# Low halves of weight tiles: a VectorE subtraction replaced by an accumulating DMA

## The chip, the cores and the metric

The kernel runs on one core of a Trainium2 chip. The metric is the device time of one execution in microseconds (us), a median over runs. Engines: PE (TensorE matmuls; PEld is its weight load), ACT (ScalarE), DVE (VectorE), POOL (GpSimd) and SP (SyncE, which here only issues DMAs). Sixteen DMA engines move all data.

## The reference

One decoder layer on a float32 input of 256 positions by 2048 channels:

```
h = rmsnorm(x); z = h @ w_in                      # 2048 x 7176
a, hb, c = conv module(z), mLSTM(z), gMLP(z)      # 512, 1024, 512 channels
x = x + concat(a, hb, c) @ w_out                  # 2048 x 2048
hm = rmsnorm(x) @ w_up                            # 2048 x 8192
x = x + square(relu(hm)) @ w_down                 # 8192 x 2048
out = rmsnorm(x)
```

## The kernel before

All weights are cut on the host into **tiles** (the code's `pieces`) of 128 x 2048 floats, 1 MB each: 64 for the mixer (numbers 0 to 63), then for each of four quarters `q` of the hidden width 16 tiles of `w_up` and 16 of `w_down`. The `w_up` tiles have numbers 64 + 32q to 79 + 32q; each is one block of 128 columns with all 2048 rows. Two neighbours fill one accumulator in PSUM, and `g` counts these pairs: tile 64 + 32q + 2g and the odd one after it.

The products are made to near float32 precision from float32r operands. Every weight is split into `hi` (rounded to float32r) and `lo` (what is left), and three products are summed. The split is done by half tile, called a **unit** (1024 columns of the tile); unit h belongs to tile h // 2. `split_unit` lets ACT copy the unit to `hi` (L131), and DVE subtracts `hi` from the raw weights to give `lo` (L132). `load_piece` issues a tile's load on SP's queue (L103).

In an up stage `mm_t` (L201 to L226) takes a tile in two halves. The first half does 8 wide matmuls (`hi` against both parts of the activations, 512 columns, L217) and then 8 narrow ones (`lo` against the high part, 256 columns, L222); the second half does its 8 narrow ones first and its 8 wide ones last. So in the trace 16 narrow ones stand together in the middle of a tile, and 16 wide ones across the border of two tiles. After a pair the results are squared behind a ReLU (L675 to L680). In a down stage `mm_n` takes each half tile with 12 matmuls (L240 to L242).

What orders the work: there are 4 buffers for raw tiles, 5 for `hi` and 5 for `lo`. Unit h therefore takes the buffers of unit h - 5, and tile j the raw buffer of tile j - 4. `advance` runs the splits 4 units ahead of the matmuls and the loads as far ahead as buffers allow. The order of the instructions on ACT, DVE, PE and SP is set by a scheduler from priorities (a split has `high_priority(HP)`); POOL keeps program order (`IN_ORDER`). In both MLP stages POOL has nothing to do until the last quarter's closing work (L700).

Of the kernel before, what the change touches and what calls it, by code (L numbers as in the profile page):

```python
# [11 lines left out]
ALU = mybir.AluOpType  # L12
# [12 lines left out]
NQ = 4  # L25
# [5 lines left out]
UNITS = 2  # L31
# [27 lines left out]
def trunk(ctx: ExitStack, tc: tile.TileContext, x, xt, w_t, w_n, w_o, w_u, w_d, gw, gm_w, cols, rows, out):  # L59
    nc = tc.nc  # L60
# [19 lines left out]
    for q in range(NQ):  # L80
        pieces += [w_u[q * 16 + i] for i in range(16)]
        pieces += [w_d[q * 16 + i] for i in range(16)]
    raws, his, los = {}, {}, {}
    state = {"dma": 0, "split": 0, "later": {}}
    n_units = len(pieces) * UNITS
# [23 lines left out]
    def x_prep(k):  # L109
        g = lng[:, k:k + 1]  # L110
        nc.scalar.mul(xg[:, k, 0, :], xs4[:, k, :], g)
        nc.vector.scalar_tensor_tensor(out=xg[:, k, 1, :], in0=xs4[:, k, :], scalar=g,
                                       in1=xg[:, k, 0, :].bitcast(F32), op0=ALU.mult, op1=ALU.subtract)

    def split_unit():

        h = state["split"]
        state["split"] += 1
        parts = 1
        if h < 4 * UNITS:  # L120
            kn = 4 // UNITS
            for k in range(h * kn, (h + 1) * kn):
                x_prep(k)
            parts = 2 if h < P2 else 1
        raw = raws[h // UNITS][:, h % UNITS * UW:(h % UNITS + 1) * UW]
        hi = wpool.tile([P, UW], F32R, tag="hi", name=f"hi{h}")
        lo = wpool.tile([P, UW], F32R, tag="lo", name=f"lo{h}")
        n = UW // parts
        for i in range(parts):
            s = slice(i * n, (i + 1) * n)  # L130
            nc.scalar.copy(hi[:, s], raw[:, s])  # L131
            nc.vector.tensor_tensor(out=lo[:, s], in0=raw[:, s], in1=hi[:, s].bitcast(F32), op=ALU.subtract)  # L132
        his[h], los[h] = hi, lo
        if h % UNITS == UNITS - 1:
            raws.pop(h // UNITS)

    def advance(h):
        while state["dma"] * UNITS <= h + DMA_AHEAD and state["dma"] < len(pieces):
            load_piece()
        while state["split"] <= h + SPLIT_AHEAD and state["split"] < n_units:  # L140
            with tc.high_priority(HP):
                split_unit()
        for fn in state["later"].pop(h, []):
            fn()
# [488 lines left out]
    for c in range(4):  # L633
# [5 lines left out]
        for cp in range(2):  # L639
# [6 lines left out]
            for i in range(2):  # L646
                k = 4 * c + 2 * cp + i
                g = colv[:, C_LMG + k:C_LMG + k + 1]
# [141 lines left out]
```

## Time and profile before

| | |
|---|---|
| median of 3 runs | 1103.77 us (1103.71 to 1104.51) |
| profiled execution | 1103.79 us, of which its span is 1102.1 us |
| PE busy | 1089.6 us, 99% |
| DVE busy | 689.6 us, 63% |
| ACT busy | 530.7 us, 48% |
| POOL busy | 57.8 us, 5% |
| moved by DMA | 211.05 MB, mean 191 GB/s |

The span is the profiled stretch of the execution. Busy shares are means over it; whether an engine sets the time is seen from who waits for whom in a stretch. Idle time of an engine that nobody waits for costs nothing.

### The profile page before, as it was taken

The numbers are of one execution on the slowest core, as the hardware profiler recorded it, in microseconds if no ns is written. First come the engines' busy times: TensorE is split into PE (matmuls) and PEld (weight loads), VectorE is DVE, ScalarE is ACT, GpSimd is POOL, SyncE is SP. The second block draws the span as 40 slices with busy tenths as digits, with TensorE's granted clock in tenths as the row PEclk, the third lists the DMA queues.
The fourth block names the chain that finished last, engine by engine and source line by source line (L and its number), as shares of the span: only waits on it lengthen the run. The fifth ranks groups of instructions, "written<-read, shape, count | busy, mean of one in ns | idle before, by whom it ended". The sixth has DMA issues, their size and how long they took to land.

```text
span 1102.1 us, 13677 instructions
## 1 busy us (share of the span) xinstructions
PE 1089.6 (99%) x5447; PEld 924.1 (84%) x5447; DVE 689.6 (63%) x841; ACT 530.7 (48%) x655; POOL 57.8 (5%) x70
## 2 busy tenths in 40 slices
PE   9999999999999999999999999999999999999997
PEld 7888888888888888888888888888888888888885
DVE  7788999665665556555546565555565555565553
ACT  7574755444564454443334443334444334444442
POOL 1002120040300000000000000000000000000111
PEclk9999999999999999999999999999999999999999
DMA  9645445554475555555555555555555555555531
GB/s 347 261 172 179 167 163 190 182 191 169 175 305 186 180 189 186 187 183 194 194 210 184 186 178 193 196 197 202 186 189 180 194 198 205 189 183 177 196 141 76
DMA packets 32176, 211.05 MB, mean 191 GB/s; under 512 B 3697, under 2 KB 4081, under 8 KB 7665
## 3 DMA queue, kind: packets, MB, share of 16 engines
q1 hardware_dynamic: 32112, 210.19, 54.1%
q8 instruction: 42, 0.69, 0.3%
q14 instruction: 22, 0.17, 0.0%
HBM read 208.08 MB, written 2.10 MB: 191 GB/s over the span
## 4 chain that ended last, share of the span: by engine, by line
PE 90%; DVE 5%; issue 3%; POOL 1%; ACT 1%; DMA 0%; SPq 0%; ACTq 0%; POOLq 0%; DVEq 0%
PE up L217 21%; PE up L222 11%; PE dn L242 10%; PE dn L241 10%; PE dn L240 10%; PE wo L240 3%; PE wo L242 3%; PE wo L241 3%; PE qk L217 2%; DVE lo L132 2%; DVE cvo L313 2%; PE o L240 1%; PE o L242 1%; PE o L241 1%; PE v L241 1%
## 5 line engine op out<-in xcount | busy, mean ns | idle before, releaser
L132 DVE TENSOR_TENSOR lo<-raw,hi 128x1024 fp32r<-128x1024 f32 (+1 forms) x388 | 474.6, 1226 | 340.8 <-ACT hi L131 340.6
L131 ACT CAST hi<-raw 128x1024 fp32r<-128x1024 f32 (+1 forms) x388 | 402.8, 1042 | 449.7 <-PE dn L242 188.7
L217 PE MATMUL up<-x,hi 128*128 128x512 f32 x1024 | 245.6, 391 | 0.0
L217 PEld LDWEIGHTS up<-x,hi 128*128 128x128 f32 x1024 | 188.0, 188 | 36.2
L240 PE MATMUL dn<-hi,u 128*128 128x512 f32 x480 | 186.7, 389 | 0.0
L241 PE MATMUL dn<-lo,u 128*128 128x512 f32 x480 | 186.7, 389 | 0.0
L242 PE MATMUL dn<-hi,u 128*128 128x512 f32 x480 | 186.7, 389 | 0.0
L222 PEld LDWEIGHTS up<-x,lo 128*128 128x128 f32 x1024 | 131.4, 191 | 5.1
L222 PE MATMUL up<-x,lo 128*128 128x256 f32 x1024 | 133.0, 283 | 0.0
L241 PEld LDWEIGHTS dn<-lo,u 128*128 128x128 f32 x480 | 90.1, 188 | 18.8
L240 PEld LDWEIGHTS dn<-hi,u 128*128 128x128 f32 x480 | 90.1, 188 | 18.7
L242 PEld LDWEIGHTS dn<-hi,u 128*128 128x128 f32 x480 | 90.1, 188 | 18.7
L217 PE MATMUL qk<-xg,hi 128*128 128x512 f32 x256 | 62.4, 392 | 1.0 <-DVE qk_t L413 1.0
L217 PEld LDWEIGHTS qk<-xg,hi 128*128 128x128 f32 x256 | 46.7, 188 | 10.9 <-PE qk L217 1.8
L313 DVE SCALAR_TENSOR_TENSOR cvo<-aT,colv,cvo 128x256 f32<-128x256 f32 x120 | 53.9, 498 | 0.0
L240 PE MATMUL wo<-hi,mix 128*128 128x512 f32 x128 | 50.4, 394 | 0.0
L241 PE MATMUL wo<-lo,mix 128*128 128x512 f32 x128 | 50.1, 391 | 0.0
L242 PE MATMUL wo<-hi,mix 128*128 128x512 f32 x128 | 49.9, 390 | 0.0
L700 POOL TENSOR_TENSOR xr<-xr,fgv 128x512 f32<-128x512 f32 x6 | 9.5, 1606 | 765.9 <-ACT jf L698 765.9
L679 ACT CAST u<-u_t 128x512 fp32r<-128x512 f32 x32 | 19.9, 621 | 53.0 <-DVE u_t L678 53.0
L680 DVE TENSOR_TENSOR u<-u_t,u 128x512 fp32r<-128x512 f32 x32 | 22.1, 691 | 19.3 <-ACT u L679 19.3
L222 PEld LDWEIGHTS qk<-xg,lo 128*128 128x128 f32 x256 | 32.9, 191 | 1.3
(224 smaller groups left out, 1006.5 us busy)
## 6 DMA issues: line engine op xcount, KB each, us to landing
raw<-in_w_u SPq DMA_DIRECT2D x64, 1024.0 KB, 4.7
raw<-in_w_d SPq DMA_DIRECT2D x64, 1024.0 KB, 4.7
raw<-in_w_n SPq DMA_DIRECT2D x28, 1024.0 KB, 4.7
raw<-in_w_t SPq DMA_DIRECT2D x16, 1024.0 KB, 4.7
raw<-in_w_o SPq DMA_DIRECT2D x16, 1024.0 KB, 4.8
raw<-in_w_n SPq DMA_DIRECT2D x6, 512.0 KB, 7.6
xr<-in_x SPq DMA_DIRECT2D x2, 1024.0 KB, 6.5
out<-xr SPq DMA_DIRECT2D x8, 256.0 KB, 2.6
```

Source lines behind the costliest of these rows:

```text
L131: nc.scalar.copy(hi[:, s], raw[:, s])
L132: nc.vector.tensor_tensor(out=lo[:, s], in0=raw[:, s], in1=hi[:, s].bitcast(F32), op=ALU.subtract)
L217: nc.tensor.matmul(pt[:, i, :], lhsT=hi[:, kk, :], rhs=act[:, k, :, :], start=(k == 0), stop=(k == NK - 1))
L222: nc.tensor.matmul(pt[:, i, 0:T], lhsT=lo[:, kk, :], rhs=act[:, k, 0, :], start=False, stop=False)
L240: nc.tensor.matmul(pt[t], lhsT=xh, rhs=hi[:, kk, :], start=(k == 0), stop=False)
L241: nc.tensor.matmul(pt[t], lhsT=xh, rhs=lo[:, kk, :], start=False, stop=False)
L242: nc.tensor.matmul(pt[t], lhsT=xl, rhs=hi[:, kk, :], start=False, stop=(k == NK - 1))
L313: nc.vector.scalar_tensor_tensor(out=o, in0=a, scalar=w, in1=o, op0=ALU.mult, op1=ALU.add)
L679: nc.scalar.copy(u[:, 2 * g:2 * g + 2, 0, :], tt)
L680: nc.vector.tensor_tensor(out=u[:, 2 * g:2 * g + 2, 1, :], in0=tt, in1=u[:, 2 * g:2 * g + 2, 0, :].bitcast(F32), op=ALU.subtract)
L700: nc.gpsimd.tensor_tensor(out=xr[:, t, cs], in0=xr[:, t, cs], in1=fgv[:, cs], op=ALU.mult)
```

## The change

For the odd `w_up` tile of each pair (32 tiles, 64 units) the low part is no longer a DVE subtraction. ACT writes the negated weights, rounded to float32r, into `lo` by a second pass over the raw unit, and a DMA from POOL's queue then adds the raw unit onto `lo` in place: -round(w) + w. The even `w_up` tiles, all `w_down` tiles and the mixer's tiles are split as before.

```
+    summed = {64 + q * 32 + 2 * g + 1 for q in range(NQ) for g in range(8)}
...
+        if h // UNITS in summed:
+            nc.scalar.copy(hi, raw)
+            nc.scalar.mul(lo, raw, -1.0)
+            nc.gpsimd.dma_start(out=lo, in_=raw, accum_op=ALU.add)
+            his[h], los[h] = hi, lo
+            if h % UNITS == UNITS - 1:
+                raws.pop(h // UNITS)
+            return
```

The numbers of matmuls and loads and their order on PE and SP stay as they are. POOL gets 64 DMA issues, which stand between its mixer work and its closing work.

ACT in the first up stage, around tiles 68 to 70, before (the number behind a name is that of the unit for `hi` and `lo` and of the tile for `raw`; what follows the underscore is internal):

```order
L131 CAST hi136_3391<-raw68_3194 128x1024
L675 COPY u_sb00_3381<-up00_3296 128x512
L131 CAST hi137_3411<-raw68_3194 128x1024
L679 CAST u0_3295<-u_t00_3383 128x2x256
L131 CAST hi138_3433<-raw69_3228 128x1024
L131 CAST hi139_3453<-raw69_3228 128x1024
L131 CAST hi140_3483<-raw70_3297 128x1024
```

The same place on ACT now (lines have moved by 10 behind the new ones):

```order
L141 CAST hi136_3395<-raw68_3194 128x1024
L685 COPY u_sb00_3385<-up00_3298 128x512
L141 CAST hi137_3415<-raw68_3194 128x1024
L132 ACTIVATE lo138_3438<-raw69_3228 128x1024
L689 CAST u0_3297<-u_t00_3387 128x2x256
L131 CAST hi138_3437<-raw69_3228 128x1024
L131 CAST hi139_3458<-raw69_3228 128x1024
L132 ACTIVATE lo139_3459<-raw69_3228 128x1024
L141 CAST hi140_3489<-raw70_3299 128x1024
```

The odd tile 69 gets two more passes: that of its first unit stands ahead of its `hi` copies, that of its second unit behind them.

DVE at the same place before:

```order
L132 TENSOR_TENSOR lo136_3392<-raw68_3194,hi136_3391 128x1024
L677 TENSOR_TENSOR u_t00_3383<-up00_3296,u_sb00_3381 128x512
L132 TENSOR_TENSOR lo137_3412<-raw68_3194,hi137_3411 128x1024
L678 SCALAR_TENSOR_TENSOR u_t00_3383<-u_t00_3383 128x512
L680 TENSOR_TENSOR u0_3295<-u_t00_3383,u0_3295 128x2x256
L132 TENSOR_TENSOR lo138_3434<-raw69_3228,hi138_3433 128x1024
L132 TENSOR_TENSOR lo139_3454<-raw69_3228,hi139_3453 128x1024
L132 TENSOR_TENSOR lo140_3484<-raw70_3297,hi140_3483 128x1024
```

And now:

```order
L142 TENSOR_TENSOR lo136_3396<-raw68_3194,hi136_3395 128x1024
L687 TENSOR_TENSOR u_t00_3387<-up00_3298,u_sb00_3385 128x512
L142 TENSOR_TENSOR lo137_3416<-raw68_3194,hi137_3415 128x1024
L688 SCALAR_TENSOR_TENSOR u_t00_3387<-u_t00_3387 128x512
L690 TENSOR_TENSOR u0_3297<-u_t00_3387,u0_3297 128x2x256
L142 TENSOR_TENSOR lo140_3490<-raw70_3299,hi140_3489 128x1024
```

The two subtractions of tile 69 are gone; nothing else has moved.

SP's loads before, with what each waits for (DVE and ACT by their names; DMAHW is a DMA of SP's queue, DMASW one of POOL's):

```order
L103 DMA raw100_4518<-in_w_u 128x2048 [waits DMAHW7_49,DVE_49]
L103 DMA raw101_4552<-in_w_u 128x2048 [waits DMAHW0_49,DVE_49]
L103 DMA raw102_4590<-in_w_u 128x2048 [waits DMAHW1_49,DVE_49]
L103 DMA raw103_4632<-in_w_u 128x2048 [waits DMAHW2_49,DVE_49]
L103 DMA raw104_4682<-in_w_u 128x2048 [waits DMAHW3_49,DVE_49]
```

And now:

```order
L105 DMA raw100_4534<-in_w_u 128x2048 [waits DMAHW7_49,DVE_49]
L105 DMA raw101_4568<-in_w_u 128x2048 [waits DMASW1_49,DMAHW0_49,DMASW0_49,Activation_49]
L105 DMA raw102_4608<-in_w_u 128x2048 [waits DMAHW1_49,DVE_49]
L105 DMA raw103_4650<-in_w_u 128x2048 [waits DMASW3_49,DMAHW2_49,DMASW2_49,Activation_49]
L105 DMA raw104_4702<-in_w_u 128x2048 [waits DMAHW3_49,DVE_49]
```

The load that takes an odd tile's buffer now waits until both accumulating DMAs of that tile have landed, where it waited for DVE before.

## Rows read from the trace of the kernel before

**Rows 1.** The page: busy time by engine; granted clock in 40 slices, in tenths.

```profile
PE 1089.6 (99%) x5447; PEld 924.1 (84%) x5447; DVE 689.6 (63%) x841; ACT 530.7 (48%) x655; POOL 57.8 (5%) x70
PEclk9999999999999999999999999999999999999999
```

**Rows 2.** Busy time by stretch (from:to, length, engines): one up stage, one down stage.

```profile
core 0: us, PE busy (x) PEld busy (x) DVE busy (x) ACT busy (x) POOL busy (x), PEclk, DMA share, GB/s
...
832.00:919.00 87.00, 87.00 (x385) 72.06 (x384) 46.13 (x43) 34.67 (x34) 0.00 (x0) 1.00 0.55 190
919.00:1008.00 89.00, 89.00 (x513) 78.64 (x512) 52.61 (x54) 41.32 (x47) 0.00 (x0) 1.00 0.55 192
```

**Rows 3.** Waits from 391 to 1008 us: first and last of 8.

```profile
DVE lo L132 <- ACT hi L131: 240.8, 183, 2.5
...
ACT hi L131 <- ACT x L649: 1.0, 1, 1.0
```

**Rows 4.** Chain that ended last, second up stage: start, length, what.

```profile
591.61 3.65 PE up L217 x16
595.26 1.91 PE up L222 x16
...
602.75 3.65 PE up L217 x16
606.40 1.91 PE up L222 x16
```

**Rows 5.** Timeline of ACT there: start, length, instruction, idle before and releaser.

```profile
592.73 0.62 ACT L679 CAST u<-u_t 128x512 fp32r<-128x512 f32 x1 [1.89 <-DVE u_t L678]
593.53 1.05 ACT L131 CAST hi<-raw 128x1024 fp32r<-128x1024 f32 x1 [0.18 <-PE up L217]
595.36 1.05 ACT L131 CAST hi<-raw 128x1024 fp32r<-128x1024 f32 x1 [0.77 <-PE up L217]
```

**Rows 6.** Timeline of DVE there.

```profile
594.62 1.23 DVE L132 TENSOR_TENSOR lo<-raw,hi 128x1024 fp32r<-128x1024 f32 x1 [0.54 <-ACT hi L131]
596.44 1.22 DVE L132 TENSOR_TENSOR lo<-raw,hi 128x1024 fp32r<-128x1024 f32 x1 [0.59 <-ACT hi L131]
600.19 1.23 DVE L132 TENSOR_TENSOR lo<-raw,hi 128x1024 fp32r<-128x1024 f32 x1 [2.52 <-ACT hi L131]
...
603.15 0.68 DVE L678 SCALAR_TENSOR_TENSOR u_t<-u_t 128x512 f32<-128x512 f32 x1
```

**Rows 7.** Timeline of SP's queue there.

```profile
597.69 0.33 SPq L103 DMA_DIRECT2D raw<-in_w_u  x1
```

**Rows 8.** Groups of instructions by form: count, busy, mean ns of one.

```profile
L132 DVE TENSOR_TENSOR lo<-raw,hi 128x1024 fp32r<-128x1024 f32 x380 | 469.4, 1238 | 338.8 <-ACT hi L131 338.7
L131 ACT CAST hi<-raw 128x1024 fp32r<-128x1024 f32 x380 | 398.2, 1051 | 447.8 <-PE dn L242 188.7 <-PE up L217 135.5 <-PE wo L242 36.6
...
L700 POOL TENSOR_TENSOR xr<-xr,fgv 128x512 f32<-128x512 f32 x6 | 9.5, 1606 | 765.9 <-ACT jf L698 765.9
```

**Rows 9.** DMA issues: count, size of one, median us to landing.

```profile
raw<-in_w_u SPq DMA_DIRECT2D x64, 1024.0 KB, 4.7
...
raw<-in_w_n SPq DMA_DIRECT2D x6, 512.0 KB, 7.6
...
out<-xr SPq DMA_DIRECT2D x8, 256.0 KB, 2.6
```

**Rows 10.** Line L103: time from issue to landing of its 188 loads.

```profile
DMA to landing us min/median/max: 4.5/4.7/10.5
```

**Rows 11.** Busy time by stretch, start of the kernel (columns as in rows 2).

```profile
18.00:23.00 5.00, 5.00 (x24) 4.14 (x23) 5.00 (x8) 3.68 (x6) 0.00 (x0) 1.00 1.05 423
23.00:28.00 5.00, 5.00 (x24) 4.14 (x23) 3.40 (x6) 4.78 (x6) 0.00 (x0) 1.00 1.02 425
```

## The prediction

> **What bounds the kernel now.** I read the busy times first, then the busy times of the MLP's stages apart, then who waits there, and then one period of an up stage instruction by instruction. PE is busy 99% of the span at a granted clock that reads 9 in every slice [rows 1]. That alone proves little, so the stages come next: an up stage has PE busy 89.00 of 89.00 us, a down stage 87.00 of 87.00, both at clock 1.00, which is the upper of its two levels (2.4 GHz), while DVE is busy 52.6, ACT 41.3 and the DMA engines 55% [rows 2]. The list of waits from 391 to 1008 us has eight entries, and in none of them does PE wait: DVE waits for ACT, ACT for buffers that PE frees [rows 3]. So in the stretch that the change touches PE works without a gap, and everything else runs ahead of it by as much as five buffers allow. The question is how far ahead each `lo` is, and whether the new way still fits.
>
> **The lead of a low part, before.** In the chain, 16 wide matmuls take 3.65 us and 16 narrow ones 1.91 [rows 4], so a tile takes 5.56 us and a pair 11.13 (from one row to the one of the same kind two tiles on: 602.75 - 591.61 is 11.14). The wide run from 591.61 straddles a border at its middle, 593.44: an odd tile begins. Two tiles on, at 604.57, the next odd tile begins; its first `lo` is read from 606.40, and its second from the middle of that narrow run, 607.36. Its `hi` copies on ACT start at 593.53 and 595.36 [rows 5], its subtractions on DVE end at 595.85 and 597.66 [rows 6]. The leads are 10.6 and 9.7 us.
>
> **What goes.** 64 subtractions of 1.24 us [rows 8], 79 us of DVE. PE waits for none of them, so their going gains nothing. I see no room for a gain in an up stage, since PE has no idle time there to give back.
>
> **What ACT gets.** 64 more passes over 128x1024, which I price like a `hi` copy at 1.05 us [rows 8]: 67 us in all, 16.8 in each up stage, where ACT is idle 47.7. What hides it is that idle time, and I checked the place of each pass. The first unit's pass needs a `lo` buffer that PE has read by 591.61 (five units earlier, the end of the preceding narrow run); it runs from about 591.7 to 592.75, in the 1.89 us that ACT stood idle before 592.73 [rows 5], and holds the cast behind it by hundredths. The second needs a buffer whose narrow matmuls end at 596.21 (half of the run from 595.26) and stands behind the copy that ends at 596.41, so it ends at 597.46. Nothing more follows on ACT until 599. Cost: nothing.
>
> **What the DMAs cost.** They can be issued at 592.75 and 597.46, so they have 13.6 and 9.9 us to land before PE reads at 606.40 and 607.36. No row shows an accumulating DMA or a DMA issued by POOL. Bounds: below, SP's issue of 0.33 us [rows 7] and a 256 KB store's 2.6 [rows 9], together 2.9 us; above, POOL's 1.6 us for a whole tensor operation [rows 8] and three trips of 512 KB (two reads and a write one after the other) at the slowest median landing in the list, 7.6 us [rows 9], together 24.4. A gain is excluded at the lower end, as PE has no gap to give back. I take the value nearest to a row: an add of 512 KB has to read two operands of 512 KB, as many bytes as a tile's load, which lands in 4.7 us [rows 9]; with 1.6 for POOL that is 6.3 us. If a tile's load runs beside it, its 1.05 MB take another 2.5 us at the 423 GB/s that the engines held from 18 to 23 us [rows 11]: 8.8 us. Both are under 9.9. At the upper end 14.5 us would be missing for each of 32 odd tiles, 464 us.
>
> **Whether the engines have room.** A pair loads two tiles, 2.10 MB, and now adds 2 x 0.52 MB. Counted as two passes (both operands read) the pair moves 4.19 MB in 11.13 us, 377 GB/s, 89% of 423. One pass makes 283 GB/s, three make 471, which is over what any row shows. The point at which it breaks is 2.5 passes. I take two.
>
> The Trainium skill (Collectives: The Full Stack, section "The bandwidth ceiling: the fold count and why AG ≠ RS ≠ AR") states that an adding transfer runs at about half the rate of a copying one, because it reads two sources over one ring, and that the add itself costs no cycles. No run here shows such a transfer. By that rule the pair would need 9.9 us of the engines at 423 GB/s, my two passes, and the chance of the first rival below would be a tenth.
>
> **Who else waits.** SP's load of the tile four on waits for both adds to land. It was issued at 597.69 [rows 7]; now at 597.46 plus 6.3 to 8.8, at the latest 606.3, landing 4.7 later at 611.0. Its first reader is ACT's first pass of the odd tile two pairs on, 591.7 + 22.3 = 614.0. That leaves 3 us, and the even tile's load queued behind it on SP (DVE frees that buffer near 603.2, the end of the subtraction one tile after that at 597.66) loses at most those 3 us of its own distance. On POOL only other adds stand behind an add, and the closing multiplications (L700) come long after. DVE, ACT and PE wait for nothing new except PE for the adds.
>
> **Sum.** Against the profiled execution, 1102.1 us of span and 1.69 around it, 1103.79: minus 0 (DVE), plus 0 (ACT), plus 0 (adds landing inside 9.9 us). I predict **1103.8 us**; the median of the runs, 1103.77, is the same to 0.02.
>
> **Rivals.**
>
> *The engines run full.* For it: 89% is near the edge, and a read-modify-write may count its write as well. Against it: loads and adds differ in place and could overlap better than two loads do. At three passes a pair takes 12.39 us, 1.26 too many; over the 8 pairs of an up stage that is 10.1 us, of which the 3 us of slack take a part, and the down stage (55% full) restores the slack. 7 us by 4 quarters is 28: 1132 us. At four passes it is 14.9 us for a pair, 27 us a quarter: 1212. Chance 0.24, half for each.
>
> *The add lands too late.* Slower by one mechanism: PE stands at L222 of each odd tile until its second `lo` has landed, and as the buffers of the next unit are freed later by the same time, nothing is made up. It decides from 9.9 us on and costs 32 us for each microsecond beyond. For it: some tile loads took up to 10.5 us to land [rows 10], though most of those in a stretch with full engines; with POOL's 1.6 that is 12.1, 2.2 us too late, 70 us in all: 1174 us. Against it: engines free for 45% of the stage. Chance 0.17.
>
> *POOL is held by DVE.* The longest unbroken run of DVE in a pair is from 600.19 to 603.83 [rows 6], 3.6 us. If POOL could issue nothing in such a run, the 8.8 us would become 12.4, 2.5 us too late: 80 us, 1184. Against it: the issues fall at 592.8 and 597.5, outside this run, and DVE's two subtractions next to them are gone. Chance 0.03. The Trainium skill (SBUF — State Buffer, section "SBUF: two separate sides") describes such a lock: while DVE runs in a two-port mode, GpSimd can't write the descriptors of its DMAs; the section "Who interferes with whom" adds that a two-input tensor operation takes only the read side, and those are the ones here. No row shows POOL and DVE in each other's way.
>
> *Faster after all.* A stall of PE that the list of waits doesn't show and that DVE causes. Against it: 89.00 of 89.00. About 1101 us, chance 0.03.
>
> **How the numbers follow.** No change 0.53, engines full 0.24, too late 0.17, POOL held 0.03, faster 0.03. A measurement of this kernel tells 0.2%, 2.2 us, from no change, so: faster 0.03, same 0.53, slower 0.44. The likeliest case by itself lies between 1103 and 1106. The range has to reach into the slower cases until a fifth is left out: up to 1190 it holds the three passes, the late add at its price and the held POOL; four passes (0.12) and later landings (about 0.05) stay outside, and a faster result (0.03) below 1102.
>
> **What the profile will show.** If I am right: 64 DMA issues on POOL; up stages still 89 us long with PE at 89; no wait of PE for `lo`; DMA share near 0.9 to 1.0 in an up stage and 0.55 in a down stage as now; DVE near 33 us and ACT near 58 in an up stage. Time from an add's issue to landing under 9.9 us. I am wrong if PE or its weight loads wait for a DMA into `lo` (too late, in each odd tile alike), or ACT for a DMA into `raw` (engines full, growing from the first pair of a quarter to the eighth), or if up stages keep their length while the time moves.

## The result and the profile after

The changed kernel takes 1110.38 us (median of 4 runs, 1110.14 to 1114.0) where the kernel before took 1104.14 on the same chip: 0.6% or 6.2 us slower, ratio 1.0064 with the interval [1.0043, 1.0085]. The time lies in the predicted range, but the likeliest case, no change, did not come. The same kernel, run again beside the experiments, gave 1.0058 [1.0045, 1.0072]. The profiled execution was the longest of its runs both times: its span is 1112.3 us, the spans of the other three are 1108.4 to 1108.7. So the trace shows about 10 us of loss, and the other executions about 6.4.

The page of after, busy times and DMA queues (packets, MB, share of 16 engines over the span), beside [rows 1]:

```profile
PE 1093.7 (98%) x5447; PEld 925.2 (83%) x5447; DVE 611.1 (55%) x777; ACT 594.3 (53%) x719; POOL 113.8 (10%) x134
...
q1 hardware_dynamic: 32112, 210.19, 54.1%
q0 software_dynamic: 9216, 33.56, 15.3%
```

DVE lost 64 instructions and 78.5 us, ACT and POOL each gained 64, and the adds, on the queue q0, take 15.3% of the DMA engines' time.

Busy time by stretch in after: the first, second, third and fourth up stages (each stretch as long as the up stage of [rows 2], which has the same columns):

```profile
core 0: us, PE busy (x) PEld busy (x) DVE busy (x) ACT busy (x) POOL busy (x), PEclk, DMA share, GB/s
391.00:480.00 89.00, 85.33 (x488) 74.72 (x487) 34.56 (x45) 55.07 (x66) 12.21 (x14) 1.00 0.94 252
567.00:656.00 89.00, 88.11 (x499) 77.14 (x498) 33.30 (x38) 55.70 (x61) 13.95 (x16) 1.00 0.99 265
743.00:832.00 89.00, 88.34 (x501) 77.40 (x500) 32.50 (x38) 56.74 (x61) 13.95 (x16) 1.00 0.97 262
919.00:1008.00 89.00, 88.26 (x494) 77.14 (x493) 31.94 (x36) 56.40 (x62) 13.98 (x16) 1.00 0.96 258
```

DVE and ACT stand where the prediction put them (near 33 and 58 us). PE is no longer busy all the time, at an unchanged clock of 1.00, and the DMA engines went from a share of 0.55 to 0.94 and more. From the first matmul of an up stage to the first of the down stage behind it, the four up stages took 90.08, 89.06, 89.07 and 89.07 us before, and 94.87, 90.72, 90.41 and 90.43 after. That is 9.2 us; with 1.0 us by which the first of them begins later, it is the whole difference of the two spans (1112.3 - 1102.1 = 10.2). That 1.0 us is not the change's: the first `qk` matmul of the mixer already starts at 56.7 us in place of 55.7, far ahead of the first add at 385 us, and in the other traces of this case it starts between 55.4 and 56.8.

Waits in after from 391 to 1020 us (who for whom, us in total, times, longest), where [rows 3] has none of PE:

```profile
PEld up L232 <- DMA lo<-raw: 8.2, 11, 1.4
...
PE up L232 <- DMA lo<-raw: 5.8, 9, 1.2
...
ACT lo L132 <- DMA raw<-in_w_u: 2.4, 2, 1.4
```

PE and its weight loads now wait for the accumulating DMA, 11 times for at most 1.4 us. ACT's wait for a tile's load, the sign of loads that fall behind, is there only twice. Where PE stands is seen in its timeline in the first up stage (start, length, instruction, idle before and releaser):

```profile
443.01 1.11 PE L232 MATMUL up<-x,lo 128*128 128x256 f32 x8
445.17 1.22 PE L232 MATMUL up<-x,lo 128*128 128x256 f32 x8 [1.05 <-DMA lo<-raw]
446.23 3.82 PE L227 MATMUL up<-x,hi 128*128 128x512 f32 x16
449.89 2.08 PE L232 MATMUL up<-x,lo 128*128 128x256 f32 x16
451.80 3.82 PE L227 MATMUL up<-x,hi 128*128 128x512 f32 x16
455.45 1.11 PE L232 MATMUL up<-x,lo 128*128 128x256 f32 x8
457.77 1.21 PE L232 MATMUL up<-x,lo 128*128 128x256 f32 x8 [1.20 <-DMA lo<-raw]
```

The narrow run of an even tile is one piece of 16 (449.89). That of an odd tile is cut in two, and the gap is always before its second half: the second unit of the tile, whose lead the prediction put at 9.9 us. The first unit, with 13.6 us, is never waited for.

The 9.9 us count from the end of ACT's pass. POOL begins to issue 0.3 us after that (the pass of the add at 614.93 ends at 614.63), and the second half's matmuls would have begun near 624.5 (half of a run of 1.91 us behind 623.51), so a landing counted from POOL's issue has about 9.5 us. Waits begin there: the add issued at 969.88 landed after 9.69 us and held the weight load for 0.24. The chain that ended last says how long such a second add took (second up stage; start, length, what):

```profile
602.20 5.46 DMA raw<-in_w_u
...
614.93 10.02 DMA lo<-raw
...
625.08 5.28 DMA raw<-in_w_u
...
637.82 10.04 DMA lo<-raw
...
647.90 1.21 PE up L232 x8
```

The add that POOL begins to issue at 614.93 lands after 10.02 us, and PE starts to read at 624.99. The chain, which before ran through PE alone in this stretch [rows 4], now runs from one landed add over the load that its buffer was kept from, to the next second add. What stood beside that add is on the timelines of POOL and of SP's queue:

```profile
610.28 0.87 POOL L133 DMA_DIRECT2D lo<-raw  x1 [5.99 <-ACT lo L132]
614.93 0.87 POOL L133 DMA_DIRECT2D lo<-raw  x1 [3.78 <-ACT lo L132]
621.41 0.87 POOL L133 DMA_DIRECT2D lo<-raw  x1 [5.61 <-ACT lo L132]
626.06 0.87 POOL L133 DMA_DIRECT2D lo<-raw  x1 [3.78 <-ACT lo L132]
```

```profile
613.26 0.83 SPq L105 DMA_DIRECT2D raw<-in_w_u  x2
```

The two adds of a tile are 4.65 us apart, about the 4.7 that were forecast. Just ahead of the second, at 613.26, SP issues two loads at once: the odd tile's, which had waited for the adds of the tile four before, and the even tile's behind it in the queue. So the second add shares the engines with the end of the first add and with two loads. The landings show it: the first adds of these pairs (610.3, 621.4, 633.2) took 5.2 to 6.0 us, the second adds (614.9, 626.1, 637.8) 9.8 to 10.0, over all 64 from 4.7 to 12.2 with a median of 7.5.

### The profile page after: what moved, and what is told of

Read it like the earlier page. It is cut to its first block, busy times and chain, and to the rows that moved or that the text cites. A ratio compares the mean times of both kernels' runs of the same rounds, so it can differ in the third digit from the quotient of the medians.

```text
span 1112.3 us, 13893 instructions
## 1 busy us (share of the span) xinstructions
PE 1093.7 (98%) x5447; PEld 925.2 (83%) x5447; DVE 611.1 (55%) x777; ACT 594.3 (53%) x719; POOL 113.8 (10%) x134
## 3 DMA queue, kind: packets, MB, share of 16 engines
q0 software_dynamic: 9216, 33.56, 15.3%
## 4 chain that ended last, share of the span: by engine, by line
PE 76%; DMA 12%; issue 7%; DVE 2%; POOL 1%; ACT 1%; SPq 0%; POOLq 0%; ACTq 0%; DVEq 0%
PE up L227 11%; PE dn L250 10%; PE dn L252 10%; PE dn L251 10%; DMA lo<-raw 8%; PE up L232 6%; PE qk L227 4%; DMA raw<-in_w_u 3%; PE wo L250 2%; PE wo L251 2%; PE wo L252 2%; PE qk L232 2%; PE o L250 1%; PE o L252 1%; PE o L251 1%
## 5 line engine op out<-in xcount | busy, mean ns | idle before, releaser
L142 DVE TENSOR_TENSOR lo<-raw,hi 128x1024 fp32r<-128x1024 f32 (+1 forms) x324 | 396.1, 1226 | 406.9 <-ACT hi L141 406.7
L141 ACT CAST hi<-raw 128x1024 fp32r<-128x1024 f32 (+1 forms) x324 | 335.6, 1040 | 380.2 <-PE dn L252 176.6
L232 PEld LDWEIGHTS up<-x,lo 128*128 128x128 f32 x1024 | 132.1, 191 | 13.5 <-DMA lo<-raw 8.2
L232 PE MATMUL up<-x,lo 128*128 128x256 f32 x1024 | 136.2, 284 | 6.0 <-DMA lo<-raw 5.8
L133 POOL DMA_DIRECT2D lo<-raw x64 | 56.0, 875 | 645.7 <-ACT lo L132 627.2
L132 ACT ACTIVATE lo<-raw 128x1024 fp32r<-128x1024 f32 x64 | 67.6, 1058 | 31.5 <-PE up L232 20.5
L131 ACT CAST hi<-raw 128x1024 fp32r<-128x1024 f32 x64 | 67.0, 1047 | 28.9 <-PE up L227 27.9
L227 PEld LDWEIGHTS qk<-xg,hi 128*128 128x128 f32 x256 | 46.7, 188 | 10.8 <-PE qk L227 1.8
```

The costliest lines, as they stand in the source:

```text
L131: nc.scalar.copy(hi, raw)
L132: nc.scalar.mul(lo, raw, -1.0)
L133: nc.gpsimd.dma_start(out=lo, in_=raw, accum_op=ALU.add)
L227: nc.tensor.matmul(pt[:, i, :], lhsT=hi[:, kk, :], rhs=act[:, k, :, :], start=(k == 0), stop=(k == NK - 1))
L232: nc.tensor.matmul(pt[:, i, 0:T], lhsT=lo[:, kk, :], rhs=act[:, k, 0, :], start=False, stop=False)
```

## The experiments

The theory after the comparison: the whole loss is that second adds land later than their lead of 9.9 us (about 9.5 from POOL's issue), because the engines are nearly full beside them. Its rivals: the engines are over their capacity and loads fall behind (then no earlier issue helps); the new work on ACT and POOL costs by itself; or the spacing of the adds, two in one tile and none in the next, is what costs.

### The same kernel again

> The changed kernel once more, to see how its loss spreads over executions and over the four up stages. Theory A (an add's landing is stretched by the loads that share the sixteen DMA engines, and the second add of an odd tile, whose lead is only 9.9 us, then misses it): 1108 to 1114 us, PE waiting at L232 for an add of the second unit only, most in the first up stage. Theory B (an accumulating DMA takes about 10 us by itself, whatever runs beside it): a like stall in every odd tile, 0.2 to 0.3 us in each. Theory C (the extra passes on ScalarE or late loads hold PE): waits of PE for ScalarE, or of ScalarE for a load, make up the loss.

1111.23 us (5 runs, 1109.93 to 1113.8), ratio 1.0058 [1.0045, 1.0072]. The landings of its adds reach up to 13.1 us:

```profile
DMA to landing us min/median/max: 4.7/7.9/13.1
```

The loss is there again at the same size, with 7.5 us of waits of the weight loads, in 12 places; the up stages are 95.35, 90.61, 90.05 and 90.97 us long. In the first of them one wait of 2.33 us of PE is followed by matmuls at a lower clock (shown in the last section), so there the loss is more than the waits.

### Adds for the first unit of every tile

```diff
-    summed = {64 + q * 32 + 2 * g + 1 for q in range(NQ) for g in range(8)}
+    summed = {64 + q * 32 + g for q in range(NQ) for g in range(16)}
...
-        if h // UNITS in summed:
+        if h // UNITS in summed and h % UNITS == 0:
```

> The first unit of every w_up tile gets its low part by an add, the second unit of every tile by VectorE: as many adds, passes and bytes as in the changed kernel, but every add has the long lead (13.6 us by the working of the prediction) and one is issued every 5.6 us in place of two within 4.7. Theory A with the lead as what is missed: no PE wait for an add, 1104 to 1105 us, though the engines are as full. If the engines' capacity itself is short (a pair needs more than 11.1 us of them), the loads fall behind and 1107 to 1112 us remain. Theory B: landing about 10 us as before, inside 13.6, so 1104. Theory C: as slow as the changed kernel, 1108 to 1112.

1104.35 us, ratio 1.0001 [0.9992, 1.001]: no loss, with as many adds and as full engines. Second up stage and landings of this kernel:

```profile
567.00:656.00 89.00, 89.00 (x514) 78.66 (x513) 35.72 (x40) 55.74 (x60) 12.18 (x14) 1.00 0.98 284
```

```profile
DMA to landing us min/median/max: 5.0/7.5/10.8
```

A share of 0.98 does not hold PE up by itself. The slowest add took 10.8 us, too long for a second unit and short enough for a first. But this edit changes the spacing as well as the lead, so the next one keeps the spacing and takes the other unit.

### Adds for the second unit of every tile

```diff
-        if h // UNITS in summed:
+        if h // UNITS in summed and h % UNITS == 1:
```

(with the 16 tiles of a quarter in `summed`, as above)

> The second unit of every w_up tile gets its low part by an add, the first by VectorE: bytes, passes and the even spacing (one add each 5.6 us) as in first_units, but each add has only the short lead (9.9 us) that the second unit of an odd tile has in the changed kernel. If the short lead is what costs: adds land as in first_units (median 7.5, some over 9.9), so PE waits for some of them, 1106 to 1112 us. If it is the pairing of two adds and two loads in one place that makes an add land after 10 us: 1104 to 1105, landing under 9.9.

1118.71 us (6 runs, 1109.78 to 1121.59), ratio 1.0121 [1.0094, 1.0147]. The adds are spaced as evenly as in the experiment before, and the loss is twice that of the change, so the spacing is not what costs. That 64 instead of 32 adds now have the short lead fits the factor of two. Its waits and landings:

```profile
PEld up L232 <- DMA lo<-raw: 5.3, 8, 1.7
```

```profile
DMA to landing us min/median/max: 4.4/7.7/11.6
```

The profiled execution was the fastest of the six, 1109.78 us, so the trace shows a loss of 5.7 us only, by which its up stages are longer (93.51, 90.36, 89.85 and 89.28 us); the other five took 1116 to 1122 and left no trace. Four of these five have a mean granted clock of 0.995 or 0.996 where the profiled one has 0.998. In the change the profiled execution was the longest. How late an add lands in full engines differs between executions, and by what is not settled.

The trace also shows that late adds need no loads that are let go together. Here each load waits for one add, and except in the last 8 us of an up stage SP issues the loads at least 2.1 us apart, where the change has pairs 0.42 us apart; still adds land after up to 11.6 us, and PE waits for them.

### Half as many adds

```diff
-    summed = {64 + q * 32 + 2 * g + 1 for q in range(NQ) for g in range(8)}
+    summed = {64 + q * 32 + 2 * g + 1 for q in range(NQ) for g in range(1, 8, 2)}
```

> Only the odd tiles of every second pair are made by adds: 32 adds in place of 64, each with the same lead as in the changed kernel. Theory A: the engines are busy about 0.8 in an up stage, landing falls to 6 to 8 us, PE waits under 1 us in all, 1104 to 1105 us. Theory B: landing as before, half the loss, 1107. Theory C: half the loss, 1107.

1104.11 us, ratio 1.0 [0.9991, 1.0008]. The second units have the same lead as in the change, but the engines have room (a share of 0.77), and no add takes longer than 7.4 us:

```profile
567.00:656.00 89.00, 89.00 (x514) 78.67 (x512) 43.18 (x46) 49.32 (x55) 6.96 (x8) 1.00 0.77 238
```

```profile
DMA to landing us min/median/max: 4.4/5.7/7.4
```

### Half as many loads

```diff
     def load(j):
+        if j in summed:
+            raws[j] = raws[j - 1]
+            return
```

> The odd w_up tiles aren't loaded; they are split from the raw buffer of the even tile before (so they hold that tile's weights). The adds stay as in the changed kernel. Theory A: with half the loads gone the engines are busy 0.7 to 0.8 in an up stage, the second add lands in 5 to 7.5 us, PE waits for none: 1104 to 1105. Theory B (the add's own time): landing of the second add near 10 us still, loss as before, 1108 to 1112.

1104.19 us, ratio 1.0 [0.9991, 1.0009]. All adds are there, and PE waits for none of them. They land within 9.9 us (median 5.7) at a DMA share of 0.75 to 0.78; the longest are first units, which have 13.6 us, and no second unit's add takes longer than 7.1. Together with the experiment before: to take away half of either stream is enough.

### Copies instead of adds

```diff
-            nc.gpsimd.dma_start(out=lo, in_=raw, accum_op=ALU.add)
+            nc.gpsimd.dma_start(out=lo, in_=raw)
```

> The same DMAs from GpSimd's queue without the add: raw is copied onto lo (lo then holds the rounded weights, so the product is another one). One operand read in place of two. Theory A with two passes for an add: the DMA's share of the engines falls by about half (from 15% to 8% of the span), landing to 5 to 6.5 us, no PE wait, 1104 to 1105 us. If what counts is the queue of GpSimd and not the second read, share, landing and loss stay: 1108 to 1112 us.

1104.75 us, ratio 1.0005 [0.9996, 1.0015]. The same bytes written from the same queue, without the add, and no wait of PE:

```profile
q0 software_dynamic: 9216, 33.56, 8.5%
```

A copy of 512 KB takes 8.5% of 1102.9 us over 64, 1.46 us of all 16 engines; an add 15.3% of 1112.3 over 64, 2.66 us, and at half as many adds, where the engines had room, 7.7% of 1102.7 over 32, 2.65. An add costs 1.8 copies. Pairs of loads, most of them 0.42 us apart, are there in this run too, and cost nothing at its share of 0.79 to 0.80.

### The passes on ACT alone

```diff
-            nc.gpsimd.dma_start(out=lo, in_=raw, accum_op=ALU.add)
```

> The changed kernel without the adds (lo holds the negated rounded weights, so the product is another one): ScalarE's 64 extra passes stay. Theories A and B: 1104 to 1105, PE waits for nothing in the up stages. Theory C (ScalarE's passes cost): 1107 or more.

1104.16 us, ratio 0.9999 [0.999, 1.0008], ACT busy 55.9 us in an up stage and PE without a gap. So ACT's 64 passes cost nothing, and DVE's 64 missing subtractions give nothing. With POOL's 64 issues, which cost nothing in the run with both adds early (below), the second rival falls.

### The adds into buffers that nobody reads

```diff
+            sp = work.tile([P, UW], F32R, tag=("sg", "gv")[h % 2], name=f"sp{h}")
...
-            nc.scalar.mul(lo, raw, -1.0)
-            nc.gpsimd.dma_start(out=lo, in_=raw, accum_op=ALU.add)
+            nc.scalar.mul(sp, raw, -1.0)
+            nc.gpsimd.dma_start(out=sp, in_=raw, accum_op=ALU.add)
+            nc.vector.tensor_tensor(out=lo, in0=raw, in1=hi.bitcast(F32), op=ALU.subtract)
```

> All subtractions are back on VectorE, and ScalarE's extra passes and the adds go on beside them into two spare buffers that nobody reads: all the added traffic, all of ScalarE's added work, raw buffers held until the adds have landed, but PE waits for no add. If PE's wait for the second add is the whole loss: 1104 to 1105 us. If late loads or ScalarE's passes cost by themselves: 1106 to 1110.

1108.44 us (4 runs), ratio 1.0037 [1.0024, 1.0049]: mixed. The last three up stages are 89.06, 89.06 and 89.07 us long, as before the change, with all adds running beside them at a share of 0.92 to 0.94. The first took 94.19, 4.1 more, and there the expectation missed. What PE waits for at that place is not a DMA:

```profile
392.76 0.69 PE L656 MATMUL x2T<-ident,xr 128*128 128x128 f32 x2 [2.43 <-DVE xr L650]
```

DVE comes late to the residual at the start of the stage: it begins it at 392.02, behind two subtractions of an odd tile for which it had waited 6.08 us. After the gap PE's granted clock averages 0.69 from 393 to 398 us, which takes a part of the 4.1. This belongs to the experiment, not to the change, in whose trace no such gap stands.

### Both adds issued with the first unit

The deciding one. Both passes and both adds of an odd tile are issued with the tile's first unit, into a sixth `lo` buffer; bytes, count and engines stay.

```diff
-        lo = wpool.tile([P, UW], F32R, tag="lo", name=f"lo{h}")
         if h // UNITS in summed:
+            for i in range(UNITS if h % UNITS == 0 else 0):
+                lo = wpool.tile([P, UW], F32R, tag="lo", name=f"lo{h + i}", bufs=W_BUFS + 1)
+                part = raws[h // UNITS][:, i * UW:(i + 1) * UW]
+                nc.scalar.mul(lo, part, -1.0)
+                nc.gpsimd.dma_start(out=lo, in_=part, accum_op=ALU.add)
+                los[h + i] = lo
...
-            nc.scalar.mul(lo, raw, -1.0)
-            nc.gpsimd.dma_start(out=lo, in_=raw, accum_op=ALU.add)
-            his[h], los[h] = hi, lo
+            his[h] = hi
...
+        lo = wpool.tile([P, UW], F32R, tag="lo", name=f"lo{h}", bufs=W_BUFS + 1)
```

> The changed kernel with a sixth lo buffer, and both of an odd tile's negating passes and adds issued with its first unit: the same adds of the same tiles, the same bytes, but the second add is issued about 3.7 us sooner (lead 13.5 in place of 9.9 us). If the lead of the second add against a landing of 10 us is the whole loss: no PE wait for an add, 1104 to 1105 us, with landing (10 us or more for the second add) and engine share as in the changed kernel. If full engines cost by late loads whatever the lead: 1107 to 1112.

1104.26 us, ratio 0.9999 [0.999, 1.0008]; the up stages are 90.08, 89.07, 89.06 and 89.07 us long, those of before. Second up stage, then the landings:

```profile
567.00:656.00 89.00, 89.00 (x513) 78.65 (x513) 35.35 (x40) 54.64 (x61) 12.21 (x14) 1.00 1.00 286
```

```profile
DMA to landing us min/median/max: 4.8/9.3/12.1
```

The engines are fuller than in the change (1.00 in this stage), the adds take longer (median 9.3 against 7.5), and PE waits for none of them: the longest landing, 12.1 us, is inside the lead of about 13.5. So the engines carry the whole load, and the first rival falls. The sixth buffer comes along with the earlier issue here and was not tried by itself, but the adds for first units lost nothing with five. What the change lost is the difference between landing and lead at the second unit, with what a long wait costs in clock behind it.

### The loads let go one by one

The adds read a copy that DVE makes, so that loads need not wait for them. This asks whether the two loads that SP lets go together are what makes the second add slow in the change. A first try had two copies' buffers, a second had four and made the copy later:

```diff
+            sp = work.tile([P, UW], F32, tag=("sg", "gv")[h % 2], name=f"sp{h}")
...
+            nc.vector.scalar_tensor_tensor(out=sp, in0=raw, scalar=0.0, in1=raw, op0=ALU.mult, op1=ALU.add)
...
-            nc.gpsimd.dma_start(out=lo, in_=raw, accum_op=ALU.add)
+            nc.gpsimd.dma_start(out=lo, in_=sp, accum_op=ALU.add)
```

> The changed kernel, but each add reads a spare copy of the raw unit (made by VectorE, two buffers), so that a raw buffer is free once the engines have read it and SP's load of the tile four on no longer waits for the adds to land. The same adds, the same leads. Theory A1 (a load that is let go by a late add goes out together with the even tile's load behind it, just ahead of the next second add, which then has two loads and an add beside it and lands after 10 us, and so on): loads go out 5.6 us apart, the second add lands in 7 to 9 us, no PE wait, 1104 to 1105 us. Theory A2 (the engines are full, whoever waits): the loss stays, 1107 to 1112.

1218.7 us, ratio 1.1051 [1.1024, 1.1077]. The edit failed as an experiment: DVE waits in its order until an add frees a copy's buffer, and everything behind it on DVE waits too.

```profile
DVE sp L133 <- DMA lo<-sp: 205.6, 33, 8.7
```

The second try has four buffers and `in0=hi.bitcast(F32)` in the copy, so that DVE makes it after ACT's `hi`:

```diff
-            sp = work.tile([P, UW], F32, tag=("sg", "gv")[h % 2], name=f"sp{h}")
+            sp = work.tile([P, UW], F32, tag=("sg", "gv", "cvo", "aT")[(h // 4 * 2 + h % 2) % 4], name=f"sp{h}")
...
-            nc.vector.scalar_tensor_tensor(out=sp, in0=raw, scalar=0.0, in1=raw, op0=ALU.mult, op1=ALU.add)
+            nc.vector.scalar_tensor_tensor(out=sp, in0=hi.bitcast(F32), scalar=0.0, in1=raw, op0=ALU.mult, op1=ALU.add)
```

> uncoupled without the flaw that made VectorE wait for adds: four spare buffers, and the copy stands where the subtraction stood (it depends on hi). Loads do not wait for adds to land; the second add's lead is the changed kernel's (9.7 to 9.9 us), the first's 10.5. Theory A1 (late adds let two loads go at once, which make the next second add late): loads go out 5.6 us apart, second adds land in 7 to 9 us, 1104 to 1106. Theory A2 (full engines alone): second adds still land after 10, 1107 to 1112.

1171.34 us (4 runs, 1168.14 to 1174.77), ratio 1.0608 [1.0588, 1.0627]. Both expectations missed. The loads do go one by one, mostly 5.5 to 5.6 us apart and never less than 3.8, yet second adds land after 9.3 to 12.9 us, 27 of 32 of them after more than 10. The copy also holds the first add back until only 2 us lie between the two:

```profile
606.46 0.87 POOL L135 DMA_DIRECT2D lo<-sp  x1 [10.71 <-DVE sp L133]
608.50 0.87 POOL L135 DMA_DIRECT2D lo<-sp  x1 [1.18 <-ACT lo L134]
```

```profile
PEld up L234 <- DMA lo<-sp: 50.3, 16, 4.0
```

So one disturbance was traded for another. That late adds come without paired loads is shown by the adds for second units; whether the pairs make the second adds of the change later than mere fullness would stays open.

## Why the prediction was right and wrong

**Right: what goes, and what ACT gets.** Both were priced at nothing, and the passes alone measure 0.9999. PE had no gap to give back.

**Right: which places decide.** The second unit of an odd tile, with a lead of 9.9 us. PE waits there and nowhere else, and the chain shows 10.02 us of landing that ended a wait. 64 POOL issues came as written, and DVE's 33 and ACT's 56 us near the 33 and 58 that were expected.

**Wrong, the step that failed: "If a tile's load runs beside it, its 1.05 MB take another 2.5 us ...: 8.8 us. Both are under 9.9."** The second adds of the pairs shown landed 9.8 to 10.0 us after POOL's issue, which is 10.1 to 10.3 on the prediction's count from the end of ACT's pass; others took up to 12.2 from the issue. Two things in that estimate were too small. It put one load beside the add; the trace has two loads, let go together just ahead of it, and the end of the first add. And it took the engines' rate from the kernel's start, 423 GB/s [rows 11]. The rate for this stage was in another row: 192 GB/s at a share of 0.55 [rows 2], which is 349 GB/s while busy, or 3.0 us for a tile. With the measured prices, from the two loads' issue at 613.26, two loads of 3.0 us, the add's own 2.66 and what is left of the first add (at most 2.66) end between 621.9 and 624.6; it landed at 624.95. This is an estimate: the share that the pairing has in it is not shown, since second units' adds come late without pairs too. The margin was an estimate of 8.8 against 9.9, and its own error of 1.3 to 1.5 us was larger than that.

**Wrong in size, by the same row: the engines at 89%.** Two passes was right: an add takes 1.8 copies' time, near the factor of two that the Trainium skill gives for the adding transfers of collectives (Collectives: The Full Stack, section "The bandwidth ceiling: the fold count and why AG ≠ RS ≠ AR"). But 4.19 MB at 349 GB/s take 12.0 us, more than the 11.13 of a pair, and with the measured prices (two loads of 3.0 us, two adds of 2.66) it is 11.3. The up stages stand at 0.94 to 0.99 here and at 0.96 to 1.01 with both adds early: full to the brim, and the work still gets done in time. It is not throughput that fails. With both adds early PE keeps its 11.13 us for a pair; what fullness costs is latency, and latency counted only where a lead was short.

**The rivals.** What came is "the add lands too late", with "the engines run full" as the reason. The late add was priced with 32 adds 2.2 us late (70 us); the trace has 11 waits of 0.75 us on average (8.2 us), and each of them cuts a run of narrow matmuls in two. The full engines were priced at 28 us and more. That the measured time lies in the range is therefore partly luck: the range reached up to 1190 us for the sake of rivals priced at 28 to 80 us, while the sum itself, 1103.8 us, missed by 6.6. The loads kept up: ACT waited for one twice. The lock between DVE and POOL did not show: POOL's issues took 0.87 us in the median and at most 1.07, with DVE busy for a third of the stage. "Faster" is excluded by the passes alone and by half the adds.

**Who else waits.** SP's load did wait for the adds, up to 12.8 us and 32 times; it was foreseen, and its slack of 3 us held except in two places. That the same wait would send two loads off together, into the next second add, was not seen.

No version beats the kernel before. The three that keep the adds in use and lose nothing (adds for first units, half as many adds, both adds early) equal it: PE is at 89.00 of 89.00 us in all three, and the work taken from DVE was never on its path.

## What to carry to other kernels

Before moving work onto DMAs, take the rate that the engines hold from the stage in question, bytes per second divided by the share of time that they are busy there, and not from the fastest stretch of the kernel. If the sum comes near full, count latency and not bandwidth: list which transfers can stand in the engines at the same time, and compare the landing in that company to the shortest lead, not to the median one. An operation with a price near its lead can be cured by issuing it earlier: here 3.7 us were enough, with all bytes still moved, and half as many adds or half as many loads did no better.

## What the runs showed of the hardware

- **An accumulating DMA costs 1.8 times a copy** of the same size in memory on the chip: 2.65 against 1.46 us of all 16 engines for 512 KB, both at a share of about 0.8. In fuller engines it is 2.66 (the change) to 2.87 (adds into buffers that nobody reads). POOL needs 0.87 us to issue one and 0.54 for a copy.
- **Engines at a share of 1.00 lost nothing in throughput but much in evenness:** landings of one and the same transfer went from 4.8 to 12.1 us, where they went from 4.4 to 7.4 at a share of 0.77.
- **A long stall of PE is followed by a lower clock.** In the second try at single loads, PE stood still for 3.75 us; the following 16 wide matmuls took 5.17 us where 3.82 is usual, and the granted clock averages 0.71, between the two levels (1.2 and 2.4 GHz), in these 5 us:

```profile
621.41 1.49 PE L234 MATMUL up<-x,lo 128*128 128x256 f32 x8 [3.75 <-DMA lo<-sp]
622.70 5.17 PE L229 MATMUL up<-x,hi 128*128 128x512 f32 x16
```

```profile
622.70:627.70 5.00, 5.00 (x17) 4.00 (x17) 0.51 (x1) 1.53 (x2) 0.00 (x0) 0.71 1.00 256
```

  In the second execution of the change that was traced (the run "again"), PE stood still for 2.33 us, and the granted clock averages 0.69 from 447.2 to 452.0 us:

```profile
446.05 1.54 PE L232 MATMUL up<-x,lo 128*128 128x256 f32 x8 [2.33 <-DMA lo<-raw]
447.39 5.10 PE L227 MATMUL up<-x,hi 128*128 128x512 f32 x16
```

  In the first one, where PE stood still for at most 1.2 us at a time, the clock stayed at 1.00. So a late transfer can cost more than its lateness.
